# The later modulation units summed over row blocks on VectorE, and the first chunk's decays made during the v projections

## The chip, the cores and the metric

One core of one Trainium2 chip runs the whole program in one launch. The metric is device time in microseconds (us), as the median of several executions of the same kernel. The engines are TensorE (PE), VectorE (DVE), ScalarE (ACT), GpSimd (POOL) and SyncE (SP, which issues most DMAs).

## The reference, cut to what matters

Two layers; 256 latent and 256 context tokens, width 1024. Each layer modulates, mixes by three branches (gated delta net, RG-LRU, differential attention), and ends in a SwiGLU block. In the second layer the context tokens are only an input to the mixer.

```python
s_lat = jax.nn.silu(c)
s_ctx = jax.nn.silu(c_ctx)[None]
for l in range(DEPTH):
    need_ctx = l < DEPTH - 1
    mod_l = jnp.split(s_lat @ w_mod[l] + b_mod[l], 6, axis=-1)
    mod_c = jnp.split(s_ctx @ w_mod[l] + b_mod[l], 6, axis=-1)
    u_l = modulate(rmsnorm(h_lat, norm_mix[l]), mod_l[0], mod_l[1])
    u_c = modulate(rmsnorm(h_ctx, norm_mix[l]), mod_c[0], mod_c[1])
    y_c, y_l = mixer_sublayer(u_c, u_l, ...)
    h_lat = h_lat + mod_l[2][:, None] * y_l
    h_lat = h_lat + mod_l[5][:, None] * swiglu(modulate(rmsnorm(h_lat, norm_ffn[l]), mod_l[3], mod_l[4]), ...)
    ...  # the same for h_ctx where need_ctx
return rmsnorm(h_lat, norm_final)
```

The modulation is a product of two vectors (latent, context) with a 1024 x 6144 matrix in each layer. Inside the delta net, the decay of a chunk of 128 tokens is

```python
g = jnp.cumsum(to_chunks(g), axis=-1)
diff = g[..., :, None] - g[..., None, :]
decay = jnp.where(incl, jnp.exp(jnp.where(incl, diff, 0.0)), 0.0)
lower = jnp.where(strict, jnp.einsum('nbhid,nbhjd->nbhij', kb, k) * decay, 0.0)
q_in = q * jnp.exp(g)[..., None]
```

## The kernel before, in words

**Slabs.** Every weight matrix is cut into slabs of 1024 x 128. `slab` loads one (SP's queue, into `wr`), casts it to a rounded `wh` (L265, ACT or DVE as the lists in `how` say) and subtracts to get the rest, `wl` (L266, DVE or POOL). `gemm` (L277 to L279) then makes three matmuls for each of eight k, `wh` with the rounded activations `uh`, `wh` with their rest `ul`, `wl` with `uh`: 24 matmuls a slab. Two `wl`, three `wh` and three `wr` buffers rotate. A high priority moves loads, casts and subtractions ahead in the program order that the scheduler writes for each engine; every engine then runs its own list in order.

**Modulation.** The 6144 columns of each layer's w_mod are 24 units q of 256 columns, and 48 in all. `mod_unit` loads one unit (1 MB, `wm`), and multiplies it in eight f32 matmuls (L310), one for each block k of 128 rows: `s_act[:, k]` is 128 x 32 (two of its 32 columns hold the vectors), so that a matmul fills one strip of 32 output rows, and four k lie side by side on four strips. The trace has two instructions for each f32 matmul (x16 for a unit). ACT copies the sums out (`mev`), PE transposes them (L319), and DVE adds the four strips (L321), the bias (L322), and what else is needed. 8 units are made at the start of the program, 14 during layer 0's K and Q projections (`mods0`), 12 during its attention (stage c, `more_mods`), 4 around the second norm of layer 0's mixer (`fill` in `by_halves`), 6 during layer 1's K and Q projections, and 4 around layer 1's second norm.

**Stages of a layer, in order.** A, B and gate projections, then K, Q, V (`qkv`: a slab, a convolution of three taps on DVE and ACT, L570 to L576, L601), one LX projection, the delta stage (four chunks c, two directions d; `prep`, with the fillers of slabs between), then LX, DQ, DK, DV projections, stage c (LRU scans, 16 attention units `unit(j, qt)`), stage m (branches merged, 0.38 MB and 0.5 MB slabs), output projection and second norm (`by_halves`), and the FFN: 22 blocks f of two slabs each with DVE's L1241 and L1242, then 8 outputs m of three slabs.

**Decays.** In `prep(c)` each direction loads the chunk's log decays broadcast to all partitions (`ta<-gd`, ACT's queue), adds `bcol` on DVE (L731), exponentiates on ACT (L733, L734), multiplies q (L740, `qs`), masks on POOL (L741) and exponentiates again on ACT (L745, `tc`). DVE's `c` (L755) multiplies k times k by `tc`, and the chunk's solve starts from that.

Of the kernel before, what the change touches and what calls it, by code (L numbers as in the profile page):

```python
# [179 lines left out]
def build(tc, I, out, dbg=None):  # L180
# [110 lines left out]
    def after(ins, first):  # L291

        tc.add_manual_dep(ins.ins, first.ins.name, mybir.DependencyInfo(mybir.DependencyClass.Sync, mybir.DependencyReason.DATA))

    def mod_load(l, q, p, bufs, n=8, w=MW, wtag="wm"):

        ts = []
        for k in range(0, 8, n):
            ts.append(p.tile([128, n, w], F32, tag=wtag, name=nm("wm"), bufs=bufs))
            last = SP.dma_start(ts[-1], I["wmod"][l, k * 128:(k + n) * 128, q * w:(q + 1) * w].rearrange("(a p) c -> p a c", p=128))  # L300
        return ts, last

    def mod_unit(l, q, tag, p, bufs, n=8, w=MW, wtag="wm", etag="mev", ts=None):
        nb = w // 128
        ts, last = ts or mod_load(l, q, p, bufs, n, w, wtag)
        ps = bank(tag)[:, :w]
        with tc.high_priority(offset=60):
            for k in range(8):
                j = 32 * (k % 4)
                mm = PE.matmul(ps[j:j + 32], lhsT=s_act[:, k], rhs=ts[k // n][:, k % n], start=k < 4, stop=k >= 4,  # L310
                               tile_position=(0, j))
                if k == 0 and n < 8:
                    after(mm, last)
        ev = p.tile([128, 512], F32, tag=etag, name=nm("mev"), bufs=1)[:, :w] if etag != "mev" else \
            p.tile([128, w], F32, tag=etag, name=nm("mev"), bufs=1)
        S.copy(ev, ps)
        pt = bank(tag)[:, :w].rearrange("p (b f) -> p b f", f=128)
        for b in range(nb):
            PE.transpose(pt[:, b], ev[:, b * 128:(b + 1) * 128], ident)  # L319
        o = modT[l][:, q * nb:(q + 1) * nb]  # L320
        V.tensor_reduce(o, in_=pt.rearrange("p b (g r) -> p b r g", r=32)[:, :, 0:2], op=ALU.add, axis=AX.X)  # L321
        V.tensor_tensor(o, in0=o, in1=vc(l, "bm", q * nb, nb).unsqueeze(2).to_broadcast([128, nb, 2]), op=ALU.add)  # L322
        c, k = q * nb // 8, slice(q * nb % 8, q * nb % 8 + nb)
        i = c // 3
        if c % 3 == 1:
            V.scalar_tensor_tensor(amod[l][i][:, k], in0=o, scalar=1.0, op0=ALU.add, op1=ALU.mult,
                                   in1=vc(l, ("nm", "nf")[i], k.start, nb).unsqueeze(2).to_broadcast([128, nb, 2]))
# [978 lines left out]
```

## Time and profile before

| | |
|---|---|
| median of 3 runs | 1779.91 us (1777.34 to 1780.66) |
| profiled execution | 1784.06 us, span of the trace 1782.1 us |
| PE busy | 1687.9 us (95%) |
| DVE busy | 1003.5 us (56%) |
| ACT busy | 794.2 us (45%) |
| POOL busy | 213.9 us (12%) |
| TensorE clock granted, mean | 0.987 |

The profiled execution is one of its own; its time is 1.96 us above the span, and 4.15 us above the median. Busy times are sums over the span. A timeline gives start, duration, engine, line, operation, output <- inputs, shape and count, and in brackets the idle time before it and what ended it.

### The profile page before, as it was taken

Reading aid. Unit: us, or ns where it says so; the run is one execution under the profiler, and the core shown is the slowest. Engines: PE = TensorE matmul, PEld = TensorE weight load, DVE = VectorE, ACT = ScalarE, POOL = GpSimd, SP = SyncE. Lnnn points to the kernel's source line nnn. Section 1 sums busy time; section 2 is a strip of 40 time slices with the busy share of each in tenths; the row PEclk is TensorE's granted clock in tenths of the full one; section 3 lists DMA queues with packets and bytes.
Section 4 is the critical chain, followed back from the end, with each engine's and each line's share of the span. In section 5 each row is a group of like instructions: output and inputs, shape, how many; then the busy total and the mean of one; then the engine's idle time right before and its main releaser. Section 6 shows DMA issues by size and latency. Waiting matters only on the chain.

```text
span 1782.1 us, 29542 instructions
## 1 busy us (share of the span) xinstructions
PE 1687.9 (95%) x12066; PEld 1384.6 (78%) x12066; DVE 1003.5 (56%) x1596; ACT 794.2 (45%) x1364; POOL 213.9 (12%) x274
## 2 busy tenths in 40 slices
PE   6998999999999999899999999989999999999997
PEld 4666787655788887788888888767887788979997
DVE  5767665575453345533333237676655885765554
ACT  5565653553542233422223224657544544444443
POOL 2102100000120012211111003022101002111100
PEclk9999999999999999999999999989999999999999
DMA  9773101435233344333332344632204236555664
GB/s 336 255 254 83 43 31 37 169 118 190 95 96 96 104 145 130 116 97 100 100 95 89 107 118 153 219 114 65 61 25 133 84 109 222 188 180 180 187 179 130
DMA packets 115927, 233.12 MB, mean 131 GB/s; under 512 B 7200, under 2 KB 73644, under 8 KB 115152
## 3 DMA queue, kind: packets, MB, share of 16 engines
q1 hardware_dynamic: 106592, 226.35, 39.9%
q10 hardware_dynamic: 9200, 4.88, 1.1%
q8 instruction: 95, 1.56, 0.4%
q14 instruction: 40, 0.33, 0.1%
HBM read 228.83 MB, written 2.38 MB: 130 GB/s over the span
## 4 chain that ended last, share of the span: by engine, by line
PE 68%; issue 12%; DVE 9%; ACT 5%; DMA 4%; POOL 2%; SPq 0%; POOLq 0%; DVEq 0%; ACTq 0%
PE mm L278 10%; PE mm L279 10%; PE mm L277 10%; PE dn L279 6%; PE dn L277 6%; PE dn L278 6%; PE dn L782 2%; DMA wm<-in_wmod 2%; PE dn L796 2%; DVE wl L266 1%; PE md L310 1%; PE pp L1043 1%; PE pg L278 1%; PE pg L279 1%; PE pg L277 1%
## 5 line engine op out<-in xcount | busy, mean ns | idle before, releaser
L266 DVE TENSOR_TENSOR wl<-wr,wh 128x1024 fp32r<-128x1024 f32 (+1 forms) x291 | 359.4, 1236 | 420.0 <-PE dn L279 174.2
L265 ACT CAST wh<-wr 128x1024 fp32r<-128x1024 f32 (+1 forms) x239 | 247.3, 1035 | 430.7 <-PE mm L278 148.3
L277 PE MATMUL mm<-uh,wh 128*128 128x512 f32 (+1 forms) x1056 | 376.2, 356 | 8.3 <-DVE ro L986 2.6
L278 PE MATMUL mm<-ul,wh 128*128 128x512 f32 (+1 forms) x1056 | 374.9, 355 | 2.2 <-DVE ul L387 1.8
L279 PE MATMUL mm<-uh,wl 128*128 128x512 f32 (+1 forms) x1056 | 373.5, 354 | 3.3 <-DVE wl L266 3.3
L277 PEld LDWEIGHTS mm<-uh,wh 128*128 128x128 f32 x1056 | 202.7, 192 | 41.3 <-issue 13.6
L278 PEld LDWEIGHTS mm<-ul,wh 128*128 128x128 f32 x1056 | 202.8, 192 | 31.7 <-issue 7.5
L279 PEld LDWEIGHTS mm<-uh,wl 128*128 128x128 f32 x1056 | 202.6, 192 | 27.5 <-DVE wl L266 3.7
L279 PE MATMUL dn<-uh,wl 128*128 128x512 f32 (+1 forms) x448 | 152.1, 339 | 0.9 <-DVE wl L266 0.9
L278 PE MATMUL dn<-ul,wh 128*128 128x512 f32 (+1 forms) x448 | 152.3, 340 | 0.0
L277 PE MATMUL dn<-uh,wh 128*128 128x512 f32 (+1 forms) x448 | 152.1, 339 | 0.0
L279 PEld LDWEIGHTS dn<-uh,wl 128*128 128x128 f32 x448 | 85.5, 191 | 10.5 <-DVE wl L266 1.5
L277 PEld LDWEIGHTS dn<-uh,wh 128*128 128x128 f32 x448 | 85.6, 191 | 9.8 <-issue 0.8
L278 PEld LDWEIGHTS dn<-ul,wh 128*128 128x128 f32 x448 | 85.5, 191 | 9.5 <-issue 0.4
L283 POOL TENSOR_TENSOR hid<-ft,hid 128x512 fp32r<-128x512 f32 (+1 forms) x44 | 44.7, 1016 | 318.9 <-ACT hid L282 318.9
L265 DVE CAST wh<-wr 128x1024 fp32r<-128x1024 f32 x63 | 47.3, 751 | 45.1 <-PE mm L278 35.4
L279 PE MATMUL dn<-hid,wl 128*128 128x256 f32 (+1 forms) x198 | 62.9, 318 | 1.7 <-DVE wl L266 1.7
L277 PE MATMUL pg<-uh,wh 128*128 128x512 f32 (+1 forms) x168 | 62.0, 369 | 1.2 <-ACT ta L572 1.2
L277 PE MATMUL mm<-hid,wh 128*128 128x256 f32 (+1 forms) x198 | 62.9, 318 | 0.0
L277 PE MATMUL dn<-hid,wh 128*128 128x256 f32 (+1 forms) x198 | 62.9, 318 | 0.0
L279 PE MATMUL mm<-hid,wl 128*128 128x256 f32 (+1 forms) x198 | 62.9, 318 | 0.0
L278 PE MATMUL mm<-hid,wh 128*128 128x256 f32 (+1 forms) x198 | 62.6, 316 | 0.0
(374 smaller groups left out, 3247.9 us busy)
## 6 DMA issues: line engine op xcount, KB each, us to landing
wr<-in_w SPq DMA_DIRECT2D x284, 512.0 KB, 3.6
wm<-in_wmod SPq DMA_DIRECT2D x44, 1024.0 KB, 7.8
wr<-in_w SPq DMA_DIRECT2D x18, 384.0 KB, 4.0
r<-rd SPq DMA_DIRECT2D x5, 1024.0 KB, 5.7
ta<-gd ACTq DMA_DIRECT2D x16, 256.0 KB, 3.4
wm<-in_wmod SPq DMA_DIRECT2D x16, 256.0 KB, 4.9
w<-in_w SPq DMA_DIRECT2D x4, 640.0 KB, 9.4
h<-in_hin SPq DMA_DIRECT2D x8, 256.0 KB, 4.4
```

The lines of the kernel that those rows point to most:

```text
L265: (eh.copy if eh is S else eh.tensor_copy)(hi[:, k], r32[:, k])
L266: el.tensor_tensor(lo[:, k], in0=r32[:, k], in1=hi.bitcast(F32)[:, k], op=ALU.subtract)
L277: PE.matmul(ps, lhsT=hi[:, k], rhs=xh[:, tk], start=first and i == 0, stop=False)
L278: PE.matmul(ps, lhsT=hi[:, k], rhs=xl[:, tk], start=False, stop=False)
L279: PE.matmul(ps, lhsT=lo[:, k], rhs=xh[:, tk], start=False, stop=last and i == n - 1)
L283: (eng or G).tensor_tensor(lo, in0=y, in1=hi.bitcast(F32), op=ALU.subtract)
L310: mm = PE.matmul(ps[j:j + 32], lhsT=s_act[:, k], rhs=ts[k // n][:, k % n], start=k < 4, stop=k >= 4, tile_position=(0, j))
L782: PE.matmul(p[:, j], lhsT=lhs[:, j], rhs=rhs[:, j], start=True, stop=True)
L796: PE.matmul(p[r, d, j], lhsT=lhs[r, d, j], rhs=rhs[r, d, j], start=True, stop=True, tile_position=(64 * n, 64 * n))
L1043: PE.matmul(p[:, n], lhsT=gw[:, n, j], rhs=lx[:, j], start=True, stop=True)
```

## The change

The 8 units of the start stay as they are. The 40 others are made by the generator `mod_steps`: for each block k of 128 rows DVE multiplies the 128 x 256 piece of w_mod by the vector's value of each row and adds it to an accumulator (one for each unit and vector). Four accumulators, of two units and two vectors or, for the last 16 units of layer 1, of four units and the latent vector alone, make a group: 32 operations of DVE, then four matmuls with a 128 x 32 block of ones (one strip each), ACT's copy and two transposes. There are 16 groups. Three are made in stage c (`take` once after each scan and each attention unit), three in stage m, ten in layer 0's FFN (four steps in each block f, six in each output m). No unit is left in the K and Q stages, at the second norms, or in layer 1. The decays of chunk 0 are made during the v projections in tiles that are free then, two LX projections instead of one come before the delta stage (and two instead of three behind it), and the list of the `wl` subtractions from L990 on has POOL no longer in layer 1.

```diff
-L0MODS = 10
-AMODS = 14
...
+    def mod_out(l, q, src, nv):
...
+    def mod_turn(ps, ev, tag):
+
+        S.copy(ev, ps)
+        pt = bank(tag)[:, :MW].rearrange("p (b f) -> p b f", f=128)
+        for b in range(MW // 128):
+            PE.transpose(pt[:, b], ev[:, b * 128:(b + 1) * 128], ident)
+        return pt.rearrange("p b (g r) -> p b r g", r=32)
...
+    def mod_steps(groups, tag, accs, wm):
...
+        for a, g in enumerate(groups):
+            acc = accs[a % len(accs)]
+            at = 0
+            for l, q, nv in g:
+                for k0 in range(0, 8, n):
+                    for k in range(k0, k0 + n):
+                        for v in range(nv):
+                            x, t, c = wm[i % len(wm)][:, k - k0], acc[:, at + v], s_act[:, k, v:v + 1]
+                            if k == 0:
+                                V.tensor_scalar(t, in0=x, scalar1=c, scalar2=None, op0=ALU.mult)
+                            else:
+                                V.scalar_tensor_tensor(t, in0=x, scalar=c, in1=t, op0=ALU.mult, op1=ALU.add)
+                    load(i + len(wm))
+                    i += 1
+                    yield
+                at += nv
+            ps = bank(tag)[:, :MW]
+            with tc.high_priority(offset=60):
+                for j in range(4):
+                    PE.matmul(ps[32 * j:32 * j + 32], lhsT=ones[:, 0:32], rhs=acc[:, j], start=True, stop=True,
+                              tile_position=(0, 32 * j))
+            pt = mod_turn(ps, acc[:, 0], tag)
...
+    MODS = [[(0, q, 2), (0, q + 1, 2)] for q in range(8, 24, 2)]
+    MODS += [[(1, q, 2), (1, q + 1, 2)] for q in range(0, 8, 2)]
+    MODS += [[(1, q + i, 1) for i in range(4)] for q in range(8, 24, 4)]
...
-            mods0()
...
+        lx, dq, dk = f4(), f4(), f4()
+        qkv(W_V, 8, ALL, sv, 0)
+        later.append(lambda: to_tokens(0))
+        for d in range(2):
+            decay(0, d, v4(dk[:, d]), v4(dk[:, 2 + d]))
+            between(0, d, v4(dq[:, d]))
+        for j in range(1, 4):
             qkv(W_V + j, 8 + j, ALL, sv, j)
...
-        p = proj(W_LX, ALL)
-        flush()
...
+        for j in range(2):
+            p = proj(W_LX + j, ALL)
+            flush(1 - j)
...
+                if c > 0:
+                    decay(c, d, v4(tt("ta")), v4(tt("tb")))
+                    yield
...
-        how.update(hi=[V], lo=[V] if full else [V, G])
-        for j in range(1, 4):
+        how.update(hi=[V], lo=[V])
+        for j in range(2, 4):
...
+            mods = mod_steps(MODS[6:], "md", [fp.tile([128, 4, MW], F32, tag="mac", name=nm("mac"), bufs=2) for _ in range(2)],
...
+            take(mods, 4)
```

In layer 0's K stage PE's list before reads as follows (`pg` and `mm` are the banks of the projections, `uh` and `ul` the activations, `md` the bank of the modulation):

```order
L277 MATMUL pg_900<-uh_109,wh_902 128x512
L310 MATMUL md_619<-wm_603,s_act 32x256 x8
L278 MATMUL pg_900<-ul_110,wh_902 128x512
L279 MATMUL pg_900<-uh_109,wl_903 128x512
L277 MATMUL pg_900<-uh_111,wh_902 128x512
L319 MATMUL md_630<-cst,mev_628 128x128 x2
L278 MATMUL pg_900<-ul_112,wh_902 128x512
L279 MATMUL pg_900<-uh_111,wl_903 128x512
L277 MATMUL pg_900<-uh_113,wh_902 128x512
L278 MATMUL pg_900<-ul_114,wh_902 128x512
L310 MATMUL md_636<-wm_605,s_act 32x256 x8
```

In the same place it now reads:

```order
L270 MATMUL pg_756<-uh_109,wh_758 128x512
L271 MATMUL pg_756<-ul_110,wh_758 128x512
L272 MATMUL pg_756<-uh_109,wl_759 128x512
L270 MATMUL pg_756<-uh_111,wh_758 128x512
L271 MATMUL pg_756<-ul_112,wh_758 128x512
L272 MATMUL pg_756<-uh_111,wl_759 128x512
L270 MATMUL pg_756<-uh_113,wh_758 128x512
```

The strips and the transposes of the units are gone; the list holds the slabs' matmuls alone, and so through the whole stage.

In the FFN of layer 0 DVE's list before alternates between the subtraction of a slab and an operation of the block f:

```order
L266 TENSOR_TENSOR wl_7667<-wr_7665,wh_7666 128x1024
L1241 SCALAR_TENSOR_TENSOR ft_7656<-ft_7656,mm_7594 128x512
L266 TENSOR_TENSOR wl_7698<-wr_7696,wh_7697 128x1024
L1242 TENSOR_TENSOR ft_7656<-ft_7656,dn_7625 128x512
L266 TENSOR_TENSOR wl_7737<-wr_7735,wh_7736 128x1024
L1241 SCALAR_TENSOR_TENSOR ft_7726<-ft_7726,mm_7664 128x512
```

DVE's list after, over one block f (`mac` are the accumulators, `mwm` the pieces of w_mod):

```order
L259 TENSOR_TENSOR wl_7467<-wr_7465,wh_7466 128x1024
L1279 SCALAR_TENSOR_TENSOR ft_7436<-ft_7436,mm_7374 128x512
L345 SCALAR_TENSOR_TENSOR mac_6960<-mwm_6964,s_act,mac_6960 128x256
L345 SCALAR_TENSOR_TENSOR mac_6960<-mwm_6965,s_act,mac_6960 128x256 x4
L343 TENSOR_SCALAR mac_6961<-mwm_6962,s_act 128x256 x2
L345 SCALAR_TENSOR_TENSOR mac_6961<-mwm_6962,s_act,mac_6961 128x256 x2
L345 SCALAR_TENSOR_TENSOR mac_6961<-mwm_6963,s_act,mac_6961 128x256
L259 TENSOR_TENSOR wl_7498<-wr_7496,wh_7497 128x1024
L1280 TENSOR_TENSOR ft_7436<-ft_7436,dn_7405 128x512
L345 SCALAR_TENSOR_TENSOR mac_6961<-mwm_6963,s_act,mac_6961 128x256 x3
L345 SCALAR_TENSOR_TENSOR mac_6961<-mwm_6964,s_act,mac_6961 128x256 x4
L345 SCALAR_TENSOR_TENSOR mac_6961<-mwm_6965,s_act,mac_6961 128x256 x4
```

The sums stand between the subtractions; 16 of them come in each block f as long as groups with two vectors are made (about 13 of the 22 blocks), 8 in each block after that.

PE's list after, in the same FFN, where a group ends (`mm_7464` is a block's projection; before there were only its rows L277 to L279 here):

```order
L270 MATMUL mm_7464<-uh_6509,wh_7466 128x512
L271 MATMUL mm_7464<-ul_6510,wh_7466 128x512
L272 MATMUL mm_7464<-uh_6509,wl_7467 128x512
L353 MATMUL md_7544<-mac_6960,cst 32x256
L270 MATMUL mm_7464<-uh_6511,wh_7466 128x512
L353 MATMUL md_7544<-mac_6960,cst 32x256
L271 MATMUL mm_7464<-ul_6512,wh_7466 128x512
L353 MATMUL md_7544<-mac_6960,cst 32x256
L272 MATMUL mm_7464<-uh_6511,wl_7467 128x512
L353 MATMUL md_7544<-mac_6960,cst 32x256
L270 MATMUL mm_7464<-uh_6513,wh_7466 128x512
```

Each of the four matmuls with ones stands by itself between two matmuls of a slab. In stage m all three groups stand like this (12 places); in the FFN the ten groups stand in 34 places, where two or more sometimes lie together; in stage c the four of a group lie together (3 places).

At the start of layer 0's delta stage DVE's list before is (`sc`, `qs` of chunk 0 first, `c` its strictly lower product, `cd`, `am` the start of the solve):

```order
L731 TENSOR_TENSOR sc_1410<-bcol_783,ta_1408 128x4
L740 TENSOR_TENSOR qs_1416<-qn_590,tb_1412 128x512
L731 TENSOR_TENSOR sc_1428<-bcol_783,ta_1426 128x4
L740 TENSOR_TENSOR qs_1434<-qn_590,tb_1430 128x512
L755 TENSOR_TENSOR c_276_1449<-pg_1444,tc_1421 128x512
L265 CAST wh_3671<-wr_3670 128x1024
L755 TENSOR_TENSOR c_276_1449<-pg_1444,tc_1439 128x512
L266 TENSOR_TENSOR wl_3633<-wr_3631,wh_3632 128x1024
L820 CAST cd_1482<-c_276_1449 64x512
L766 TENSOR_TENSOR qk_1463<-pg_1458,tc_1421 128x512
L766 TENSOR_TENSOR qk_1465<-pg_1458,tc_1439 128x512
L823 TENSOR_TENSOR am_1485<-cd_1482,lv_785 128x1536 x2
```

DVE's list after, in the same place:

```order
L769 TENSOR_TENSOR qs_1219<-qn_598,f_889 128x512
L599 SCALAR_TENSOR_TENSOR f_887<-xp_1200,vec,f_887 128x512
L769 TENSOR_TENSOR qs_1221<-qn_598,f_889 128x512
L781 TENSOR_TENSOR c_227_1228<-pg_1223,f_888 128x512 x2
L708 TENSOR_TENSOR sc_1270<-bcol_675,ta_1267 128x4
L769 TENSOR_TENSOR qs_1297<-qn_598,tb_1268 128x512
L846 CAST cd_1261<-c_227_1228 64x512
L708 TENSOR_TENSOR sc_1329<-bcol_675,ta_1326 128x4
L769 TENSOR_TENSOR qs_1372<-qn_598,tb_1327 128x512
L792 TENSOR_TENSOR qk_1242<-pg_1237,f_888 128x512
L792 TENSOR_TENSOR qk_1244<-pg_1237,f_888 128x512
L849 TENSOR_TENSOR am_1264<-cd_1261,lv_677 128x1536 x2
```

Chunk 0's `sc` rows are gone from here, its `qs` and `c` read the exponentials from the scratch tile `f`, and a row of chunk 1's (`sc_1270`, which reads the loaded `ta_1267`) and its `qs_1297` now stand behind `c` and ahead of `cd`, with the second direction's pair ahead of `qk` and `am`.

## Rows read from the trace of the kernel before

**Rows 1.** Table by stretch, core 0: us, busy of each engine (instructions), PEclk, DMA share, GB/s.

```profile
62.10:145.20 83.10, 78.00 (x514) 50.81 (x513) 60.24 (x117) 50.83 (x79) 3.16 (x29) 1.00 0.76 251
145.20:160.00 14.80, 11.88 (x54) 9.61 (x53) 9.67 (x16) 7.60 (x19) 7.19 (x9) 0.88 0.53 127
376.00:462.00 86.00, 79.71 (x525) 52.23 (x522) 57.70 (x140) 32.61 (x90) 0.00 (x0) 1.00 0.46 148
503.00:700.00 197.00, 196.59 (x886) 159.41 (x884) 84.16 (x96) 60.55 (x76) 23.47 (x15) 1.00 0.37 114
740.00:1060.00 320.00, 320.00 (x1415) 264.55 (x1415) 107.58 (x120) 90.73 (x110) 28.46 (x22) 1.00 0.32 99
1111.70:1192.00 80.30, 69.95 (x435) 53.55 (x434) 60.85 (x101) 50.35 (x77) 7.92 (x32) 0.97 0.56 180
1192.00:1216.00 24.00, 21.07 (x187) 16.63 (x187) 9.93 (x17) 16.63 (x46) 9.01 (x11) 0.78 0.39 111
```

**Rows 2.** Timeline of PE in the layer-0 K stage: start, duration, row, idle before.

```profile
70.10 0.39 PE L279 MATMUL pg<-uh,wl 128*128 128x512 f32 x1
70.33 0.39 PE L277 MATMUL pg<-uh,wh 128*128 128x512 f32 x1
70.65 1.07 PE L310 MATMUL md<-wm,s_act 128*32 128x256 f32 x16
...
72.46 0.38 PE L319 MATMUL md<-cst,mev 128*128 128x128 f32 x2
...
72.92 0.39 PE L279 MATMUL pg<-uh,wl 128*128 128x512 f32 x1
```

**Rows 3.** PE's waits over the whole span: total us, times, longest.

```profile
PE dn L685 <- DVE sv L601: 8.5, 3, 4.2
...
PE dn L310 <- DMA wm<-in_wmod: 4.1, 5, 1.7
PE md L319 <- ACT mev L316: 3.8, 6, 1.0
...
PE pg L762 <- DVE c L755: 2.9, 1, 2.9
PE md L310 <- DVE modT L321: 2.6, 2, 1.6
```

**Rows 4.** Timeline of ACT at the start of the layer-0 delta stage.

```profile
149.72 0.63 ACT L733 ACTIVATE tb<-ta 128x512 f32<-128x512 f32 x1 [4.55 <-DMA ta<-gd]
```

**Rows 5.** Timeline of PE near the end of layer 1's mixer.

```profile
1562.16 0.62 PE L310 MATMUL md<-wm,s_act 128*32 128x256 f32 x2
1562.71 0.39 PE L278 MATMUL mm<-mg,wh 128*128 128x256 f32 x1
1563.03 0.62 PE L310 MATMUL md<-wm,s_act 128*32 128x256 f32 x2
```

**Rows 6.** DVE by form: count, busy us, mean ns, idle before.

```profile
L266 DVE TENSOR_TENSOR wl<-wr,wh 128x1024 fp32r<-128x1024 f32 x273 | 341.6, 1252 | 399.8 <-PE dn L279 168.4 <-PE mm L279 95.0 <-issue 83.6
...
L385 DVE SCALAR_TENSOR_TENSOR nt<-h,am,nrs 128x256 f32<-128x256 f32 x28 | 17.0, 618 | 6.4 <-ACT nrs L369 4.0 <-PE md L310 2.4
L1241 DVE SCALAR_TENSOR_TENSOR ft<-ft,mm 128x512 f32<-128x512 f32 x22 | 15.1, 688 | 4.0 <-ACT ft L1240 1.6
...
L322 DVE TENSOR_TENSOR modT<-modT,vec 128x4 f32<-128x4 f32 x48 | 9.3, 194 | 0.9
...
L576 DVE SCALAR_TENSOR_TENSOR ta<-xp,vec,ta 128x256 f32<-128x256 f32 x12 | 5.4, 481 | 0.5 <-ACT ta L572 0.3
...
L1123 DVE SCALAR_TENSOR_TENSOR pe<-pe,sm,pe 128x256 f32<-128x256 f32 x8 | 3.8, 476 | 0.1
```

**Rows 7.** Timeline of DVE in layer 0's attention.

```profile
377.82 0.46 DVE L1123 SCALAR_TENSOR_TENSOR pe<-pe,sm,pe 128x256 f32<-128x256 f32 x1
378.20 0.69 DVE L1064 TENSOR_TENSOR hs<-hs,ho 128x512 f32<-128x512 f32 x1
```

**Rows 8.** POOL by form: count, busy us, mean ns, idle before.

```profile
L266 POOL TENSOR_TENSOR wl<-wr,wh 128x1024 fp32r<-128x1024 f32 x11 | 28.6, 2598 | 102.2 <-PE mm L279 52.3 <-PE dn L279 17.9 <-issue 13.7
```

More of the change, by code (lines that the diff above doesn't have):

```diff
@@ L19 @@
 L = 2
-L0MODS = 10
-AMODS = 14
-FM = 2
 KEEP = 0
@@ L289, in build, with mod_unit @@
     gmod = [[cp.tile([128, 8, 2], F32, name=f"gm{l}{j}") for j in range(2)] for l in range(L)]
[L291 to L306, printed above, removed]
+    def mod_out(l, q, src, nv):
+        nb = MW // 128
+        o = modT[l][:, q * nb:(q + 1) * nb, 0:nv]
+        V.tensor_tensor(o, in0=src, in1=vc(l, "bm", q * nb, nb).unsqueeze(2).to_broadcast([128, nb, nv]), op=ALU.add)
+        c, k = q * nb // 8, slice(q * nb % 8, q * nb % 8 + nb)
+        i = c // 3
+        if c % 3 == 1:
+            V.scalar_tensor_tensor(amod[l][i][:, k, 0:nv], in0=o, scalar=1.0, op0=ALU.add, op1=ALU.mult,
+                                   in1=vc(l, ("nm", "nf")[i], k.start, nb).unsqueeze(2).to_broadcast([128, nb, nv]))
+        if c % 3 == 2:
+            V.tensor_scalar(gmod[l][i][:, k, 0:nv], in0=o, scalar1=0.5, scalar2=None, op0=ALU.mult)
+    def mod_turn(ps, ev, tag):
[4 more added lines that the diff above has]
+        return pt.rearrange("p b (g r) -> p b r g", r=32)
+    def mod_unit(l, q, tag, p, bufs):
+        wm = p.tile([128, 8, MW], F32, tag="wm", name=nm("wm"), bufs=bufs)
+        SP.dma_start(wm, I["wmod"][l, :, q * MW:(q + 1) * MW].rearrange("(a p) c -> p a c", p=128))
+        ps = bank(tag)[:, :MW]
         with tc.high_priority(offset=60):
@@ L309, in mod_unit @@
                 j = 32 * (k % 4)
[L310 to L327, printed above, removed]
@@ L328, in mod_unit @@
-        if c % 3 == 2:
-            V.tensor_scalar(gmod[l][i][:, k], in0=o, scalar1=0.5, scalar2=None, op0=ALU.mult)
+                PE.matmul(ps[j:j + 32], lhsT=s_act[:, k], rhs=wm[:, k], start=k < 4, stop=k >= 4, tile_position=(0, j))
+        pt = mod_turn(ps, p.tile([128, MW], F32, tag="mev", name=nm("mev"), bufs=1), tag)
+        r = p.tile([128, MW // 128, 2], F32, tag="mr", name=nm("mr"), bufs=2)
+        V.tensor_reduce(r, in_=pt[:, :, 0:2], op=ALU.add, axis=AX.X)
+        mod_out(l, q, r, 2)
@@ L331, in build, with take @@
+    MODS = [[(0, q, 2), (0, q + 1, 2)] for q in range(8, 24, 2)]
+    MODS += [[(1, q, 2), (1, q + 1, 2)] for q in range(0, 8, 2)]
+    MODS += [[(1, q + i, 1) for i in range(4)] for q in range(8, 24, 4)]
+    def take(gen, n=1):
+        for _ in range(n):
+            next(gen, None)
     class Norm:
@@ L470, in build @@
     done_sp()
-    mods = [(l, q) for l in range(L) for q in range(24)][8:]
-    def next_mod(upto, *where):
-        if mods and mods[0] < upto:
-            mod_unit(*mods.pop(0), *where)
     for l in range(L):
@@ L714, in ct @@
             return pa.tile([128, 4, 128], dtype, tag=tag, name=nm(tag), bufs=bufs)
-        gg = [[{}, {}] for _ in range(4)]
-        def spans(c):
-            return slice(c * 128, (c + 1) * 128), slice(c * 128 - TK.start, (c + 1) * 128 - TK.start)
         def prep(c):
@@ L1172, in build @@
             yb.append(split(ge, yh[:, j, O], yl[:, j, O]))
+            take(mods)
         mg = []
@@ L1189, in build @@
                         V.tensor_tensor(acc[i], in0=acc[i], in1=t, op=ALU.add)
+                take(mods, 2)
             for i in range(2):
@@ L1262, in build @@
             ffn_out(m, TK)
+            take(mods, 6)
             if not full and m in YG:
```

109 lines of the change are left out of this document (57 added, 52 removed).

## The prediction

> **What bounds the kernel now.** I read the table by stretch first, to see in which stretches PE never rests. In the merge stage (503 to 700 us) and in the FFN of layer 0 (740 to 1060 us) PE is busy for the whole stretch, and DVE for 84 of 197 and 108 of 320 us [rows 1]: there every microsecond given to PE lengthens the kernel, and one given to DVE costs nothing as long as the slabs' subtractions stay on time. In the K, Q, V stages PE is busy 78 of 83 us (layer 0) and 70 of 80 (layer 1) [rows 1]; PE leads, with DVE at 60 and 61 behind it. Then I read PE's waits: the longest among those that the change touches are those for `sv` (8.5 us in 3), for ACT's copy `mev` (3.8), for `c` (2.9) and for `modT` (2.6) [rows 3]. Last, ACT's timeline at the start of the delta stage shows its first exponential 4.55 us late for the DMA of the decays [rows 4].
>
> **What a unit costs PE now.** Slab matmuls of 512 columns follow each other by 0.23 us [rows 2]. From the start of the one at 70.33 to that at 72.92 pass 2.59 us, with five such matmuls started in between (the first, and four behind the strips), so 2.59 - 5 x 0.227 = 1.45 us go to one unit: 1.1 to the x16 strips, the rest to two transposes and their edges. I take 1.43.
>
> **What a strip costs by itself.** In layer 1 strips stood singly between slab matmuls: 0.87 us from one to the next, with one slab matmul of 256 columns between [rows 5]. That matmul alone would take about half of 0.23 (an estimate from its columns), so a lone strip takes 0.75 us from PE. The operation is of the form that the change issues: 32 output rows, 256 columns, f32, two instructions. Sixteen instructions together took 1.07 us [rows 2], so four f32 strips (eight instructions) together would take about 0.55.
>
> **The change, part by part.**
>
> *K, Q, V of layer 0.* 14 units leave: 14 x 1.43 = 20.0 us of PE's 78.0, and some 3 us of waits for `mev` and `modT` [rows 3]. What is left for PE is 58 us of slabs; DVE keeps 60.2 less 14 units of small operations (some 0.5 us a unit, an estimate: L322 takes 0.19 [rows 6], and two or three such come in each), so 53 us, and ACT loses 14 copies of 51. DVE's chain of convolutions follows each slab, so I expect some idle time of PE to come back: 4 us. Term: -19; bounds -10 (DVE's chain then sets the end) and -23.
>
> *Start of the delta stage, layer 0.* The 4.55 us that ACT waits for the decays [rows 4] now pass during the v projections, and `c` need not wait for them: the 2.9 us of PE [rows 3], and part of the slow clock behind it (0.88 in that stretch [rows 1]). But chunk 1's `sc` and `qs` now stand on DVE between `c` and `cd`; their DMA is issued once ACT is through with the v tokens, so its 3 to 4 us can hold `cd` and `am` up, and the solve of chunk 0 behind them. PE has the fillers, one slab fewer. Term: -2.5; bounds 0 and -6.5. The second LX slab that now comes ahead is only moved.
>
> *Stage c.* 12 units leave (some 10 of them, 14.3 us, inside the stretch from 376 to 462), three groups come. Of their 96 sums 64 stand in that stretch; at 0.39 us each that is 25 us on DVE, which goes from 57.7 less 5.5 to 77 of 86 us [rows 1]. The attention units pass through DVE several times, so much of PE's gain is lost to waiting for it. Term: -3; bounds -14.3 (hidden) and +8 (DVE the limit with 0.62 us a sum).
>
> *Price of a sum.* A product-and-add of 128 x 256 f32 from SBUF took 476 ns [rows 6], and the next one started 0.38 us after it [rows 7]; in the convolution, where each needs the one before, 481 ns [rows 6]; in the norm's product, 618 [rows 6]. The sums alternate between two accumulators, so I take 0.39, near the first; bounds 0.38 and 0.62.
>
> *Stage m.* Three groups, twelve lone strips: 12 x 0.75 + 3 x 0.23 (transposes) = +9.7, on a PE that never rests. DVE has 113 us to spare for 37 us of sums.
>
> *FFN of layer 0.* Ten groups in 34 places: 34 x 0.75 + 10 x 0.23 = +27.8. DVE: in a block f two subtractions (2 x 1.25), two products (2 x 0.69) [rows 6] and 16 sums make 10.1 us at 0.39, against 48 slab matmuls of 0.227, 10.9 us, and 1.2 us of strips on PE. So it stays hidden, at 83% of PE's pace. Where two accumulators' last sum is late, PE's strips wait only if the scheduler put them too early; I cost that at nothing.
>
> *Second norm, layer 0.* Four units go, 5.7 us at 1.43; in part they filled the wait for the norm, which comes back. Term: -3, bounds 0 and -6.
>
> *Layer 1, K, Q, V.* Six units, 8.6 us, and their waits: -9, bounds -4 and -10 for the reason of layer 0.
>
> *Layer 1, start of the delta stage.* The clock was 0.78 from 1192 to 1216 us [rows 1], behind a wait of 4.2 us for `sv` [rows 3] and the DMA of the decays. The decays come early and a second LX slab covers part of the wait for `sv`: -5, bounds 0 and -9.
>
> *Second norm, layer 1.* Four units, 5.7 us, and a wait of 1.6 us for `modT` [rows 3]; some of it covered a wait of the norm: -5, bounds -2 and -7.
>
> *POOL's subtractions.* 11 of 2.6 us [rows 8] go to DVE at 1.25 [rows 6], 13.8 us of DVE in layer 1, which has also lost its units; hidden: 0, bounds 0 and +5.
>
> *Sum.* -19 - 2.5 - 3 + 9.7 - 3 + 27.8 - 9 - 5 - 5 = -9.0. The profiled execution took 1784.06 us, so 1775; its time was 4.15 above the median, so the median is 1771.
>
> **A rule weighed.** Four strips that lie singly cost 3.0 us [rows 5], four together about 0.55 [rows 2]. The Trainium skill ("TensorE: Matmul & The Clock Gate", Part 3, Measured speedup vs the span model) says that matmuls on different tiles of the array overlap, so that a pack takes about as long as one of them. The trace agrees where they lie together. The Trainium skill ("TensorEngine Tiling (Array Packing)", Key Properties) says that a change of the tiling mode drains the array; the lone strips of rows 5 are what that would look like. The first rule by itself would give the sum of the second rival, the second rule mine; the order has the strips of m and the FFN mostly alone, so the row decides.
>
> **The rivals.**
>
> *DVE becomes the bound in the FFN (slower).* If a sum takes 0.62 us, a block f is 16 x 0.62 + 3.9 = 13.8 us against PE's 12.1, for 13.5 blocks: +22, so 1793. It decides from 0.51 us a sum (16 x 0.51 + 3.9 = 12.1). For it: the 618 ns of a like row [rows 6], three `wr` buffers that only a subtraction frees, and 256 KB pieces that must land on time. Against it: 476 and 481 ns, and starts 0.38 us apart. Chance 0.18.
>
> *Strips cost no more than a pack.* If a group costs some 0.5 us with its transposes wherever its strips lie, m and the FFN take 6.5 us and not 37.5: 1740. For it, the packs of rows 2; against it rows 5, of the same shape. Chance 0.1.
>
> *The K, Q, V stages do not give the time back.* If DVE's and ACT's chains set their end, layer 0 yields 10 and layer 1 4, and the starts of the delta stages nothing through chunk 1's decays in the way: 9 + 5 of the former, and some of the latter, are lost, so 1785 to 1790. For it: 53 us of DVE in some 60, two waits for `sv`. Against it: 5 us of idle PE in 83 now. Chance 0.22.
>
> **How the numbers follow.** The forecast, 1771, has a chance of 0.5, and its own range is 1758 to 1781, from the bounds of the K, Q, V stages and of stage c. A change within 0.2% (3.6 us, about what a measurement of this kernel can tell) is 1776.3 to 1783.5. Of the forecast's 0.5, 0.41 lies below, 0.08 within, 0.01 above; the first rival gives 0.18 above, the second 0.1 below, the third 0.08 within and 0.12 above with 0.02 below. Faster 0.53, same 0.16, slower 0.31. The range 1750 to 1795 leaves out the second rival and half a tenth at either end.
>
> **What would show it.** In the profile after: PE busy about 58 to 60 of some 64 us in layer 0's K, Q, V; in the FFN the table by stretch 28 us longer with PE still at 100%, and single rows of strips 0.75 us apart beyond their matmul; DVE there near 80%, the spacing of its sums near 0.39 us. If PE waits for `wl` in the FFN, the first rival holds; if the FFN is under 10 us longer, the second; if PE waits for `sv`, `kn` or `xp` among the K, Q, V slabs, the third. The forecast is wrong if the sums are much dearer than 0.39 us, if a lone strip behind a matmul of 512 columns costs other than behind one of 256, or if stage c loses more than 8 us.

## The result, and the profile after

The changed kernel took 1796.3 us (median of 4 runs, 1795.42 to 1797.23), against 1780.29 us for the kernel before beside it: a ratio of 1.0077, 95% interval 1.0058 to 1.0096. (The ratios in this document are the recorded ones, over the fast executions of both kernels on one chip, so they are not quite the quotient of two medians, 1.0090 here.) It is slower by about 0.8%, where 1771 us was forecast. Its page begins (busy us, share of the span, instructions; TensorE's granted clock in 40 slices):

```profile
span 1795.4 us, 29060 instructions
PE 1681.4 (94%) x11506; PEld 1380.5 (77%) x11506; DVE 1206.0 (67%) x2074; ACT 791.0 (44%) x1344; POOL 205.4 (11%) x266
```

PE has lost only 6.5 us of work, DVE has gained 202.5, and the span has grown by 13.3. Both kernels issue the same 7356 matmuls of slabs in almost the same order, so the start of the n-th one shows where they drift apart. The numbers are starts in the two timelines of PE (us); "difference" is what the stretch took after the change less what it took before, and "forecast" adds the terms of the prediction.

| stage, by slab matmuls | before | after | difference | forecast |
|---|---|---|---|---|
| start, 0 to 96 | 24.44 to 56.54 | 24.39 to 63.23 | +6.7 | 0 |
| layer 0: K, Q, V, delta stage, to 576 | to 304.16 | to 290.56 | -20.3 | -21.5 |
| stage c, to 960 | to 476.47 | to 471.07 | +8.2 | -3 |
| stage m, to 1824 | to 674.33 | to 679.12 | +10.2 | +9.7 |
| second norm, to 2112 | to 739.36 | to 734.73 | -9.4 | -3 |
| FFN, to 3552 | to 1062.77 | to 1088.30 | +30.2 | +27.8 |
| layer 1, to its scans, 4608 | to 1377.99 | to 1393.14 | -10.4 | -14 |
| layer 1: stages c and m, to 5664 | to 1554.12 | to 1571.93 | +2.7 | 0 |
| second norm, to 5856 | to 1592.15 | to 1606.00 | -4.0 | -5 |
| to the end of the span | to 1782.1 | to 1795.4 | -0.6 | 0 |

The borders between the first rows are not sharp. The 576th slab matmul lies inside the delta stage, because slabs of the next projections fill that stage, and the two kernels place them differently. The delta stage's last output (`oacc`) begins at 332.7 us before and at 322.2 after: counted from the 96th slab matmul up to there, the gain is 17.2 us and not 20.3, and the loss of c and m together is 15.3 and not 18.4.

The stretches of the table by stretch that answer to [rows 1] (K, Q, V stages of layer 0, from the 120th slab matmul on as there; stage c; stage m; FFN) are:

```profile
69.20:138.90 69.70, 60.41 (x277) 47.31 (x277) 56.78 (x81) 50.90 (x79) 5.89 (x33) 0.97 0.37 122
290.60:471.10 180.50, 157.22 (x688) 106.34 (x687) 135.66 (x270) 82.77 (x152) 0.00 (x0) 0.92 0.31 100
471.10:679.10 208.00, 206.97 (x895) 163.95 (x894) 127.72 (x199) 65.04 (x83) 30.63 (x17) 1.00 0.40 127
734.70:1088.30 353.60, 351.95 (x1542) 273.18 (x1541) 253.91 (x488) 97.46 (x124) 43.78 (x22) 1.00 0.55 173
```

In m and in the FFN PE is busy all but 1.0 and 1.7 us, and DVE is not the bound: the stretch is longer because PE does more. In stage c it is the other way round. DVE has gone from 103 to 136 us, PE is idle for 23 of 180 us, and the granted clock is 0.92. Before, the same slab matmuls read:

```profile
304.20:476.50 172.30, 160.65 (x874) 106.75 (x873) 103.27 (x196) 84.32 (x160) 0.00 (x0) 0.99 0.43 141
```

The waits of PE inside stage c, after the change (total us, times, longest):

```profile
PE dn L1154 <- DVE pe L1150: 6.0, 6, 2.1
PE dn L540 <- ACT sq L536: 4.9, 2, 2.5
PE dn L1159 <- ACT pT L1156: 4.0, 6, 0.7
PE pp L1069 <- DMA gw<-in_gw: 3.7, 1, 3.7
PE pp L1137 <- ACT pe L1144: 3.4, 4, 1.9
```

L1150, L1156 and L1144 are steps of the attention units: PE waits for the chain PE, ACT, DVE, ACT, PE of a softmax, whose DVE steps now queue behind sums. These three rows make 13.4 us.

Where they lie says more. Until 425 us DVE hardly rests, and from 426.9 us on PE's list holds no slab matmul for 31.6 us: six attention units stand there alone, where before the change no such gap in this stage was longer than 6.3 us.

```profile
380.00:425.00 45.00, 43.89 (x224) 29.72 (x223) 42.58 (x108) 16.57 (x44) 0.00 (x0) 1.00 0.36 114
426.90:458.50 31.60, 19.25 (x97) 11.54 (x95) 21.00 (x52) 14.70 (x35) 0.00 (x0) 0.78 0.10 34
```

12.4 of the stage's 23.3 us of idle PE lie in the second stretch. PE was busy for 3.6 of the 6.6 us from 425.0 to 431.6, and from 431.6 to 445.3 the granted clock was 0.50, the lower of its two levels.

A lone strip in the FFN (a strip matmul that stands by itself between slab matmuls), which the trace before showed in layer 1 alone [rows 5], reads in PE's timeline:

```profile
1069.72 0.62 PE L353 MATMUL md<-mac,cst 128*32 128x256 f32 x2
1070.27 0.49 PE L272 MATMUL dn<-hid,wl 128*128 128x512 f32 x1
1070.69 0.62 PE L353 MATMUL md<-mac,cst 128*32 128x256 f32 x2
1071.24 0.49 PE L270 MATMUL dn<-hid,wh 128*128 128x512 f32 x1
1071.66 0.62 PE L353 MATMUL md<-mac,cst 128*32 128x256 f32 x2
```

From one to the next pass 0.97 us; less 0.23 for the slab matmul, 0.74 us, as forecast. The sums by form, and their products of k = 0, read:

```profile
L345 DVE SCALAR_TENSOR_TENSOR mac<-mwm,s_act,mac 128x256 f32<-128x256 f32 x364 | 173.3, 516 | 6.4 <-DMA mwm<-in_wmod 3.1
L343 DVE TENSOR_SCALAR mac<-mwm,s_act 128x256 f32<-128x256 f32 x52 | 16.9, 345 | 2.0 <-DMA mwm<-in_wmod 1.9
```

At the start of the program, which the prediction costed at nothing, PE's timeline after the change has this hole:

```profile
35.00 0.39 PE L271 MATMUL mm<-ul,whi 128*128 128x512 f32 x1
37.90 0.51 PE L271 MATMUL mm<-ul,whi 128*128 128x512 f32 x1 [2.51 <-POOL ul L433]
38.25 0.62 PE L272 MATMUL mm<-uh,wlo 128*128 128x512 f32 x2
38.71 0.40 PE L270 MATMUL mm<-uh,whi 128*128 128x512 f32 x1
39.03 1.51 PE L313 MATMUL dn<-wm,s_act 128*32 128x256 f32 x12
```

The wait ends with a subtraction on POOL, which does the same work there before and after. The order in SP's queue differs. From its fifteenth DMA on it issues (`wr` are slabs, `w` and `wm` what the start needs next):

```
before: wm wm w wr wm wm w wr wm wm w wr wr
after:  wm wm wr w wr wm wm w wr wr wm wm w wr
```

Four slabs now stand ahead of the last pair of `wm`, and two before. DMA is busy there: it moved 353 to 364 GB/s from 15 to 40 us, before and after. A slab's load has a priority that moves it 300 instructions ahead in the program. With 14 units gone from the K and Q stages, 300 instructions reach further back, into the start, and the slabs pass `w` and `wm`: this is read from the code, and the run with another priority for these loads bears it out.

### The profile page after: what moved, and what is told of

Same layout as the page of the kernel before. It is cut to its first block, busy times and chain, and to the rows that moved or that the text cites. A ratio compares the mean times of both kernels' runs of the same rounds, so it can differ in the third digit from the quotient of the medians.

```text
span 1795.4 us, 29060 instructions
## 1 busy us (share of the span) xinstructions
PE 1681.4 (94%) x11506; PEld 1380.5 (77%) x11506; DVE 1206.0 (67%) x2074; ACT 791.0 (44%) x1344; POOL 205.4 (11%) x266
## 4 chain that ended last, share of the span: by engine, by line
PE 65%; issue 13%; DVE 12%; ACT 5%; DMA 3%; POOL 2%; POOLq 0%; SPq 0%; ACTq 0%; DVEq 0%
PE mm L271 10%; PE mm L272 10%; PE mm L270 10%; PE dn L272 6%; PE dn L270 6%; PE dn L271 6%; PE dn L808 2%; DVE wl L259 2%; PE pp L1069 2%; PE dn L822 2%; DVE mac L345 1%; PE md L353 1%; PE dn L919 1%; PE pg L271 1%; PE pg L272 1%
## 5 line engine op out<-in xcount | busy, mean ns | idle before, releaser
L259 DVE TENSOR_TENSOR wl<-wr,wh 128x1024 fp32r<-128x1024 f32 (+1 forms) x299 | 367.6, 1230 | 260.2 <-PE dn L272 107.8
L345 DVE SCALAR_TENSOR_TENSOR mac<-mwm,s_act,mac 128x256 f32<-128x256 f32 x364 | 173.3, 516 | 6.4 <-DMA mwm<-in_wmod 3.1
L276 POOL TENSOR_TENSOR hid<-ft,hid 128x512 fp32r<-128x512 f32 (+1 forms) x44 | 60.1, 1365 | 325.6 <-ACT hid L275 325.6
L258 DVE CAST wh<-wr 128x1024 fp32r<-128x1024 f32 x61 | 42.0, 691 | 40.8 <-PE mm L271 38.4
L272 PE MATMUL pg<-uh,wl 128*128 128x512 f32 (+1 forms) x176 | 64.2, 365 | 0.0
L271 PE MATMUL pg<-ul,wh 128*128 128x512 f32 (+1 forms) x176 | 64.1, 364 | 0.0
L270 PE MATMUL mm<-hid,wh 128*128 128x256 f32 (+1 forms) x198 | 63.2, 319 | 0.0
```

Source lines behind the costliest of these rows:

```text
L258: (eh.copy if eh is S else eh.tensor_copy)(hi[:, k], r32[:, k])
L259: el.tensor_tensor(lo[:, k], in0=r32[:, k], in1=hi.bitcast(F32)[:, k], op=ALU.subtract)
L270: PE.matmul(ps, lhsT=hi[:, k], rhs=xh[:, tk], start=first and i == 0, stop=False)
L271: PE.matmul(ps, lhsT=hi[:, k], rhs=xl[:, tk], start=False, stop=False)
L272: PE.matmul(ps, lhsT=lo[:, k], rhs=xh[:, tk], start=False, stop=last and i == n - 1)
L276: (eng or G).tensor_tensor(lo, in0=y, in1=hi.bitcast(F32), op=ALU.subtract)
```

## The experiments

Ratios are to the kernel before on the same chip, with their 95% intervals; the changed kernel itself stands at 1.0077. Places in a run are given by its slab matmuls, as in the table above.

**Stage c without most of its sums.** This leaves 84 of stage c's 96 sums out of the computation.

```diff
-                    for k in range(k0, k0 + n):
+                    for k in range(k0, min(k0 + n, ks)):
...
-            mods = mod_steps(MODS[:3], "dn", t[:1], t[1:])
+            mods = mod_steps(MODS[:3], "dn", t[:1], t[1:], 1)
```

> The changed kernel, but in stage c (layer 0's attention) each accumulator gets only its first product: 84 of the 96 sums of the three groups there are left out; their loads, strips and transposes stay. The changed kernel took 180.5 us from the 576th to the 960th slab matmul of layer 0, the one before 172.3. Theory A (the sums lengthen DVE's softmax chain, PE waits for it and its clock falls): the stretch falls to about 170 us, 10 less, and the granted clock there comes back from 0.92 to about 0.98. Theory B (PE has too little to do there once the units are gone, the sums don't matter): the stretch stays at 178 to 181 us and the clock at 0.92.

1776.01 us, ratio 0.9964 (0.9948 to 0.998). From the 576th slab matmul to the 960th:

```profile
289.80:445.50 155.70, 147.62 (x688) 100.63 (x687) 103.90 (x186) 83.41 (x153) 0.09 (x1) 0.98 0.33 113
```

That is 24.8 us less than after the change, with the same 688 PE rows: 15.2 of them are idle time of PE (23.3 to 8.1), 9.6 are PE's own busy time (157.2 to 147.6), in a stretch where the clock rose from 0.92 to 0.98. Some of it is order (fillers moved behind the 960th): to the 1152nd it is 21.3. Theory A holds, at twice the size that it expected; B falls. Slab matmuls now lie between the attention units to the end. Against the kernel before, the stretch to the 1152nd is 9.3 us shorter here (207.2 to 216.5): that is what the twelve units gave back, less the groups' strips, and the sums took 21.3. The medians say the same: this run is 20.3 us under the changed kernel.

**Half of the sums left out.** Every second product is left out of the computation, 48 of 96.

```diff
+                        if k % 2 and k >= ks[0]:
+                            continue
...
-            mods = mod_steps(MODS[:3], "dn", t[:1], t[1:])
+            mods = mod_steps(MODS[:3], "dn", t[:1], t[1:], (0, 8))
```

> The changed kernel, but in stage c only every second product is added: 48 of the 96 sums of the three groups there are left out. With 84 left out the stretch from the 576th to the 1152nd slab matmul fell from 228.4 to 207.2 us and the granted clock rose from 0.94 to 0.98. Theory A (every sum on DVE lengthens the softmax chain by its own length): about half of that, 10 to 13 us less than the changed kernel. Rival (there is a load of DVE up to which its sums cost nothing, and past it PE waits and its clock falls): nearly all of it, 17 us or more.

1780.77 us, ratio 0.999 (0.9975 to 1.0006). To the 1152nd slab matmul the stretch lost 18.1 us. So the first 48 sums that go are worth 18 us, 0.38 each, and the next 36 about 3: the rival is nearer. From 12 sums to 48 there is nearly room; from 48 to 96 each costs about its own length on DVE (0.40 us from start to start). The longest stretch of PE without a slab matmul tells the same: 8.3 us here, and 31.6 with all the sums. How much of a sum's price is the longer chain, and how much the slab matmuls that are used up too early, no run separates.

**Units back in stage c.**

```diff
+            def c_units():
+                for q in range(8, 20):
+                    mod_unit(0, q, "dn", cq, 1)
+                    yield
+
+            mods = c_units()
```

> The changed kernel, but twelve units (q 8 to 19 of layer 0) are made in stage c by eight strip matmuls each, as before the change, and none of the groups is made in stage c and in stage m; the FFN keeps its ten groups. Theory A and B both: stage c goes back to about 172 us (8 less) and stage m loses its 10 us of lone strips, so about 1778 us. If the loss in stage c came from something else that the change did (the earlier decays, the LX slab moved), the stretch stays near 180 and the time is about 1786.

1781.38 us, ratio 1.0004 (0.9989 to 1.0019). From the 576th to the 1152nd slab matmul 7.8 us went, in the rest of m 6.4: near what both theories expected. The stretch to the 1152nd is still 4.1 us longer than before the change (220.6 against 216.5), so at most that much is left for the earlier decays, the moved LX slab and the other order of slabs.

**The three groups of stage c moved to stage m.**

```diff
-            mods = mod_steps(MODS[3:6], "md", [t[:, 0:4]], [t[:, 4:6], t[:, 6:8]])
+            mods = mod_steps(MODS[:6], "md", [t[:, 0:4]], [t[:, 4:6], t[:, 6:8]])
```

> The changed kernel, with the three groups of stage c made in stage m as well: none in c, six in m, ten in the FFN as in the change. Theory A (sums cost in c because DVE stands in the softmax chain, and nothing on DVE in m, where PE never rests): c falls by 22 us, m grows by the lone strips of three groups, 3 x 3.2, so about 1783 us. Rival (DVE becomes the limit of m with 163 us of work in some 205): m grows by over 15 us, 1790 or more.

1786.51 us, ratio 1.0019 (1.0004 to 1.0035). The stretch from 576 to 1152 lost 23.8 us, though a part of m with its added strips lies in it, and the rest of m gained 10.6. The same sums that cost stage c some 20 us cost m its strips and little else.

**Strips together.**

```diff
-            with tc.high_priority(offset=60):
+            with tc.high_priority(offset=600):
...
+                    if j < 3:
+                        after(mm, end)
```

> The changed kernel, with the four strip matmuls of each group made dependent on the group's last sum and given a priority of 600 in place of 60, so that they lie together in PE's order in all 16 groups. Theory P (a strip by itself costs 0.75 us and four together about 0.55): stage m and the FFN of layer 0 get shorter by 46 x 0.75 less 13 x 0.55, that is 27 us, so about 1769 us. Rival (the strips cost the same wherever they stand, or PE now waits for the last sum instead): within 5 us of 1796.

1790.43 us, ratio 1.0056 (1.0036 to 1.0076): near the rival's number, but the trace shows two halves, a gain and a new wait. A pack that waits, and one that does not:

```profile
758.88 0.64 PE L357 MATMUL md<-mac,cst 128*32 128x256 f32 x8 [1.76 <-DVE mac L349]
...
1034.19 0.40 PE L272 MATMUL dn<-hid,wl 128*128 128x512 f32 x1
1034.52 0.64 PE L357 MATMUL md<-mac,cst 128*32 128x256 f32 x8
1035.09 0.50 PE L270 MATMUL dn<-hid,wh 128*128 128x512 f32 x1
```

The second takes 0.90 - 0.23 = 0.67 us from PE, where four lone strips take 3.0. The three groups of m waited 0.4 to 5.5 us for DVE, six of the ten in the FFN 0.5 to 1.8 us, and four did not wait.

**Strips together and late.**

```diff
+                    after(mm, lastmm[0])
+                    if j < 3:
+                        after(mm, end)
...
-                              for _ in range(4)])
+                              for _ in range(4)], 4)
```

> The changed kernel, with each group's four strip matmuls kept together and put behind the last matmul of the slab that stands ahead of them in the program; in the FFN they are issued four steps (one block f) after the group's last sum, so that PE should find the sums done. The run before kept them together but put them where PE waited 1 to 5 us for the sum in seven groups of ten; four that did not wait took 0.67 us and saved 2.2 to 3.0. Theory P (lone strips cost, a pack doesn't, the wait took the gain away): stage m and the FFN lose 13 x 2.3, some 30 us, and the time is about 1766 us. Rival (the wait for DVE's sums stays, since DVE runs later than the order assumes): 1785 or more.

1769.69 us, ratio 0.9929 (0.9906 to 0.9952), 27 us under the change. (The waits that the expectation speaks of are those above, 0.4 to 5.5 us in nine of thirteen groups.) The FFN of layer 0 now reads:

```profile
724.70:1058.60 333.90, 333.90 (x1543) 270.38 (x1542) 254.25 (x488) 95.23 (x123) 54.32 (x22) 1.00 0.59 183
```

PE has no wait left there, and DVE's 254 us are hidden. The stage costs 333.9 - 323.4 = 10.5 us for ten groups, and not 30.2. In its trace 19.7 us of the gain lie in the FFN and 5.5 in m; another 6.5 lie in stage c (173.9 us from the 576th to the 960th), where the edit changes no work, and those are not the strips'. This edit alone makes the changed kernel 0.7% faster than the kernel before.

**The start's order.**

```diff
+        slabs[0] += 1
+        early = EARLY0 if slabs[0] <= 4 else early
```

`EARLY0` is 180.

> The changed kernel, with the first four slabs' loads given a priority of 180 in place of 300, so that on SP's queue they no longer stand ahead of the start's modulation pieces (one instead of four slabs ahead of the last pair). Theory Q (the DMA queue is the bound of the start, and the slabs moved ahead of the pieces of w_mod that the first normalised blocks need): the 96th slab matmul starts at 56 to 58 us instead of 63.2, and the time is 5 to 7 us lower, about 1790. Rival (the wait is only moved, the first K slab comes later by as much): within 2 us of 1796.

1787.53 us, ratio 1.0037 (1.0019 to 1.0055). The 96th slab matmul starts 7.7 us earlier, and the lead stays to the end: theory Q. The edit moves four loads and nothing else in the code, so the place of these loads is the cause, directly or through the order that the scheduler then writes for the other engines.

**POOL's subtractions.**

```diff
-        how.update(hi=[V], lo=[V])
+        how.update(hi=[V], lo=[V] if full else [V, G])
```

> The changed kernel, with POOL back in the list of the subtractions from the LX projections on in layer 1. Theory (the 3.4 us that layer 1 lost between its 4416th and 4896th slab matmul come from DVE taking these subtractions): 3 us less, 1793. Rival (they come from elsewhere, as the second LX slab that is gone from there): within 1.5 us of 1796.

1800.06 us, ratio 1.0097 (1.0068 to 1.0126), against 1.0077 (1.0058 to 1.0096): no gain. The term of 0 stands. (Only eight of the eleven subtractions of [rows 8] lie in layer 1; POOL keeps the other three.)

**The first decays back in the delta stage.**

```diff
-        for d in range(2):
-            decay(0, d, v4(dk[:, d]), v4(dk[:, 2 + d]))
-            between(0, d, v4(dq[:, d]))
```

> The changed kernel, with the decays of chunk 0 made in the delta stage again, as before the change; the two LX slabs ahead of it stay. Theory T (the early decays are worth what the prediction said, 2.5 us in layer 0 and some of the 5 in layer 1): 4 to 7 us more, 1800 to 1803. Rival (chunk 1's decays, which now stand ahead of the solve on DVE, take it away): within 2 us of 1796.

1788.4 us, ratio 1.0036 (1.0018 to 1.0053): 7 us less without the early decays, where the theory said 4 to 7 more and the rival none. Both fall. Of the 8.2 us in the trace, 3.4 lie in layer 1 between the 4032nd and the 4608th slab matmul, 1.5 ahead of that (0.6 of them at the start of the program), and 2.8 in a stretch that nothing in this edit touches. The first of these has a likely cause in the rows. In layer 1 of the changed kernel, DVE's list at the start of the solve reads:

```profile
1220.66 0.68 DVE L781 TENSOR_TENSOR c<-pg,f 128x512 f32<-128x512 f32 x1
1222.12 0.17 DVE L708 TENSOR_TENSOR sc<-bcol,ta 128x4 f32<-128x4 f32 x1 [0.78 <-DMA ta<-gd]
1223.52 0.17 DVE L708 TENSOR_TENSOR sc<-bcol,ta 128x4 f32<-128x4 f32 x1 [1.23 <-DMA ta<-gd]
1223.71 0.83 DVE L846 CAST cd<-c 64x512 f16<-64x512 f32 x1
```

`c` is there, but `cd` stands behind chunk 1's two `sc`, and these wait 2.0 us for their DMA. The stage before is late as well: the last `sv` starts 52.5 us behind the 4032nd slab matmul, and 40.9 in the run without the early decays. Counted the same way the first `c` is 2.1 us later here, and `cd` 2.8.

**All four corrections, and two neighbours.** The next run takes four edits together: the groups of stage c in stage m, strips together and late, the start's order, and the first decays in the delta stage.

> The changed kernel with the four corrections together: no sums in stage c (six groups in stage m), strips kept together and late, the start's pieces of w_mod ahead of the slabs on SP's queue, the decays of chunk 0 in the delta stage as before the change. From the single runs: 1796 - 30 (strips, with three more groups in m at about 1 us each) - 19 (stage c) - 8 (start) - 6 (decays) gives about 1735 us, 2.6% under the kernel before. If the parts overlap (the clock of stage c and the strips of m are one loss counted twice), 1750 or more.

1741.85 us, ratio 0.9772 (0.9726 to 0.9818): 2.3% faster than the kernel before, and 43 us of span, somewhat less than the sum of the four (61 us were expected over the change, 54 came). With the early decays kept:

> As the run with the four corrections, but with the decays of chunk 0 made during the v projections, as the change does. If the early decays cost what the run without them showed, 5 to 8 us more than that one, about 1741; if that difference was chance, within 2 us of it.

1744.14 us, ratio 0.9789 (0.975 to 0.9827): within the intervals. By the end of layer 0's FFN this run was 5.6 us ahead, but only 0.9 of them at the 960th slab matmul, and the rest where the two programs do not differ; in layer 1 it lost 4.4 between the 4032nd and the 4608th. With units in stage c:

> As the run with the four corrections, but stage c makes twelve units (q 8 to 19) with eight strip matmuls each as before the change, and stage m none. By the runs so far units in c cost it 13 us over no work there, and six packed groups in m some 6: about 1742 us, 7 more than the one with six groups in m. Rival (in m DVE or the loads cost more than that): the same or less.

1749.84 us, ratio 0.9818 (0.9785 to 0.9852): some 8 us more, as expected, though the intervals overlap.

## Why the prediction was wrong

**Right: what PE got back and what the strips cost.** K, Q, V of layer 0 gave what was forecast: 83.1 us [rows 1] became 69.7 with one LX slab more in it (24 x 0.23 = 5.5 us), so 18.9 less, of 19. Together with the delta stage it is 20.3 of 21.5 by the slab matmuls, 17.2 by the stage's last output; m took 10.2 of 9.7, the FFN 30.2 of 27.8. The price of a lone strip from [rows 5], taken at 0.75, held at 0.74 behind matmuls of 512 columns, and the order's count of lone places was the right way to sum it. The second rival (strips cost no more than a pack wherever they lie) falls for the change as it was made: they pack only where they lie together, 0.67 us for four. What the Trainium skill says ("TensorE: Matmul & The Clock Gate", Part 3, Measured speedup vs the span model) agrees with those packs alone: there the four together took 0.64 us, and a lone one 0.62.

The third rival (K, Q, V do not give the time back) falls by its size, though the sign that was named for it appeared: PE waited longer for `sv` than before.

```profile
143.88 0.66 PE L685 MATMUL dn<-cst,sv 128*128 128x128 f32 x4 [2.05 <-DVE sv L601]
```

```profile
138.04 0.69 PE L693 MATMUL dn<-cst,sv 128*128 128x128 f32 x2 [4.82 <-DVE sv L624]
```

The forecast had allowed 4 us of idle PE there, so the sign alone does not tell the two apart.

**Right: DVE hides the sums in the FFN.** Sums that follow each other start 0.39 us apart in DVE's timeline ((3.24 - 0.48) / 7 for the eight at 756.29 below, of which one takes 0.48), as in the forecast, and with the strips packed PE was busy for all of 333.9 us. The first rival (DVE becomes the bound in the FFN) falls.

**Wrong: "Stage c. Term: -3".** This is the step that failed; it measured +8.2 (+1.7 to +7.2 in four more traces that leave the work of stage c and the order of its slabs as they are). The step added 25 us to DVE's busy time, got 77 of 86, and took most of that for room. But DVE stands inside the softmax chain, where PE waits for its steps, and the sums queue ahead of them; and PE's slab matmuls, which fill such waits, were used up at 426.9 us. The runs without 84 and without 48 sums show 21 and 18 us for the sums, where the step took off 11 (14.3 less 3); the units gave back 9, less the groups' strips, and not 14.3. Idle PE then cost a second time: the clock granted in the stretch was 0.92 and not 0.99, and the same 688 rows took 9.6 us more of PE. The upper bound, +8, is right by its value, but by luck: it took 0.62 us a sum, and a sum takes 0.40.

**Missing: the start.** It was taken as unchanged, because its instructions are. Its place in SP's queue is not, and DMA is busy there; the order of SP's list showed it and was not read. It cost 6.7 us.

**Wrong: the early decays.** A gain of 2.5 us and a part of 5 was forecast; without the early decays the kernel was 7 us faster, and in the corrected kernel there was no difference that the runs can tell. In layer 1 both pairs of traces show a loss with them (3.4 and 4.4 us between the 4032nd and the 4608th slab matmul), in layer 0 the two pairs differ in sign. That they gain nothing is shown. In layer 1 the rows show what the prediction itself feared for layer 0, `cd` behind chunk 1's `sc` and their DMA, and a later `sv`; why they gain nothing in layer 0, where the `sc` did not wait, is open.

**Too small: the second norm of layer 0**, -9.4 and not -3: the four units there did not cover waits. PE's busy time in the stretch fell by 9.0 us (56.3 to 47.4), 2.2 us a unit where 1.43 was taken, and its idle time stayed (8.8 and 8.3):

```profile
674.30:739.40 65.10, 56.31 (x374) 45.03 (x373) 38.12 (x66) 25.97 (x45) 22.32 (x19) 0.95 0.39 122
```

```profile
679.10:734.80 55.70, 47.36 (x302) 43.01 (x301) 37.80 (x59) 24.60 (x41) 20.36 (x19) 0.94 0.38 119
```

That this makes up for a part of the losses is luck.

**Too large: layer 1's start**, -10.4 and not -14, of which the early decays lose 3.4. The 2.7 us of layer 1's stages c and m, which were forecast unchanged, are not explained; the runs differ there by up to 4.8 us (174.0 to 178.8) with no edit in it.

Together: by the table, measured less forecast, 11.2 (stage c) + 6.7 (start) + 3.6 + 2.7 + 2.4 + 1.2 + 1.0 + 0.5 - 6.4 - 0.6 = 22.3 us lie between the forecast -9.0 and the +13.3 of the spans. Some 3 more come from the step to the median, which the forecast put 4.15 us below the profiled execution; here it was 0.9 below.

## What to carry to other kernels

Work moved to an engine with idle time is free only where no other engine waits for that engine's next step: in an FFN where PE leads the sums cost PE nothing, and in an attention stage 48 of them cost 18 us. Count how the scheduler lays out small matmuls in strips, not only how many there are; here some 25 us hung on whether four lay together and came after their inputs were ready. And when instructions are taken out of a program whose priorities count instructions, look at the queues of the stages ahead of the change too.
